# Attention values in blocks of four queries: 512-column products, a dense upper half and a spread lower half

## The chip, the cores and the metric

The kernel runs on one core of one Trainium2 chip. The metric is the device time of one execution in microseconds. A core has five engines that run their own instruction queues: PE (TensorE, matrix products and transposes), DVE (VectorE), ACT (ScalarE), POOL (GpSimd) and SP (SyncE, here only issuing DMAs). PE reads SBUF and writes PSUM, which has eight banks of 128 partitions by 512 fp32 columns.

## The reference

One layer of a hybrid decoder, on 1024 tokens of width 1024: a pre-norm, one wide input product, two groups of heads beside each other (eight heads of differential softmax attention, four heads of gated linear attention), an output product, a post-norm and the residual. The part that matters here is the differential attention:

```python
def diff_attention(q, k, v, lam):          # q,k: (B,S,H,2,64); v: (B,S,H,128)
    q = q * (DA_HEAD_DIM ** -0.5)
    def block(args):                       # one block of 128 queries
        qb, bi = args
        s = jnp.einsum('bqhmd,bkhmd->bhmqk', qb, k)
        mask = key_pos[None, :] <= q_pos[:, None]
        p = jax.nn.softmax(jnp.where(mask, s, -jnp.inf), axis=-1)
        w = p[:, :, 0] - lam * p[:, :, 1]
        return jnp.einsum('bhqk,bkhv->bqhv', w, v)
...
oa = rms_norm(oa, subln_g) * (1.0 - lam_init)
oa = oa.reshape(B, S, DA_WIDTH) * jax.nn.silu(ga)
...
y = jnp.einsum('bse,ed->bsd', jnp.concatenate([oa, ob], axis=-1), w_out)
return x + rms_norm(y, post_g)
```

## The kernel before, in words

Each fp32 product is done as three products of rounded parts (high x high, low x high, high x low). A "split" makes the two parts of a tile: ACT copies the high part, DVE subtracts it from the tile for the low part.

The first two thirds of the kernel make the projections, the gated attention, and the split weights of the output product, and leave them in DRAM. The last third, from about 637 us, is the attention stage. It is written as three streams of PE work, and `merge` interleaves them:

- `all_scores` takes the eight heads in turn and in each the eight query blocks from 7 down to 0. `scores(h, qb)` multiplies queries with keys for both maps (tile `sc`, three PSUM banks), DVE adds the mask and takes the row's extreme (L1167, with the accumulator read beside it), ACT takes the exponential (L1177), DVE the reciprocal of the row sums (L1202), POOL scales the second map (L1203), and DVE forms the weights, first map minus second (L1207). They lie in `p0`, one buffer for each query block, and `w[h, qb]` is set when that is written in the program.
- `all_values` takes the eight heads in turn. `values(h, j)` handles query blocks 2j and 2j+1 for j = 3, 2, 1, 0: `turn(g)` transposes the weights of two key tiles on PE into one of two banks (`wtr`), ACT and DVE split them (`wt_hi` L1244, `wt_lo` L1245), and `times(g)` multiplies them with the values' parts into `po`. A turn is written one turn ahead of its products. ACT copies `po` to `o`. `attn_norm` then squares `o`, splits the square, sums it over partitions by a product with ones (`ms`, in a bank of the transposes), scales by the gate and sends it to DRAM (`mixd`). It is mingled with the turns that follow.
- `out_early` multiplies what is already there with the output weights (`ypart`), as a filler, and later starts the last row tiles (`yps`).

All matmuls and transposes are issued in the order in which they are written (`tc.keep_in_program_order`). The order on the other engines is chosen by the compiler's scheduler. The merge keeps a clock for each stream: a stream has a begin, an end and a total cost, each `yield c` moves its clock by c/cost of its length, and the stream with the lowest clock goes next. A yielded function is a condition: the stream rests until it holds. The values of a pair wait for its lower block in `w`; the scores of block qb of the next head wait until the last turn of the pair that reads the same buffer has been written (`used`). Scores run from 0 to T = 288 units, 36 a head, values from LAG = 21 to T + LAG, the output products from -6 to T + LAG.

Of the kernel before, what the change touches and what calls it, by code (L numbers as in the profile page):

```python
# [14 lines left out]
P = 128  # L15
# [5 lines left out]
DA_HEADS = 8  # L21
# [10 lines left out]
def hymba_kernel(  # L32
# [21 lines left out]
    act, dve, pool, pe, sp = nc.scalar, nc.vector, nc.gpsimd, nc.tensor, nc.sync  # L54

    def fp(t):
        return t.bitcast(F32)

    def cols(half):
        return slice(half * 512, half * 512 + 512)  # L60
# [37 lines left out]
    def bank(i, shape, name):  # L98
        return psum.tile(shape, F32, tag=f"b{i}", name=name)
# [10 lines left out]
    def mm(*a, **k):  # L110
        tc.keep_in_program_order(pe.matmul(*a, **k))  # L111

    def tr(dst, src):
        tc.keep_in_program_order(pe.transpose(dst, src, ident))  # L114
# [867 lines left out]
    def chain(*streams):  # L982
        for st in streams:
            yield from st

    def load_qk(h, n, half):

        if h % 2 and (n == "k" or half):
            t = smps[0].tile([P, 2, 512], F32R, tag=f"{n}{half}", name=f"{n}{half}")
        else:  # L990
            t = kp.tile([P, 2, 512], F32R, tag=f"{n}{half}", name=f"{n}{half}")
        d = qk_d["k" if n == "k" else "q"][h][:, :, :, cols(half)]
        if n != "qs":
            sp.dma_start(fp(t), d.rearrange("m t p s -> (t p) m s"))
        else:
            for i in range(2):
                sp.dma_start(fp(t[64 * i : 64 * i + 64]), d[:, 1 - i].rearrange("m p s -> p m s"))
        qk[h, n, half] = t
# [73 lines left out]
    SC, TR, PO, Y = order_b[:3], order_b[3:5], order_b[5], order_b[6:]  # L1072
# [43 lines left out]
    def load_v(h):  # L1116
        v = [smp.tile([P, NT, P], F32R, tag="v", name=f"v{t}", bufs=4) for t in range(2)]
        for t in range(2):
            ins = sp.dma_start(fp(v[t]), v_d[h // 4][t, h % 4])
            if h == 0:  # L1120
                tc.keep_in_program_order(ins)
        return v
# [9 lines left out]
    def tr_bank(name, shape):  # L1132
        n_tr[0] += 1
        return bank(TR[n_tr[0] % 2], shape, name)


    w, used, scored, opened = {}, set(), [], {}
# [74 lines left out]
    def all_scores():  # L1212
        for h in range(DA_HEADS):
            for qb in range(NT - 1, -1, -1):
                if qb % 2 and h:
                    yield lambda h=h, qb=qb: (h - 1, qb // 2) in used
                yield from scores(h, qb)
                if qb == NT - 1 and h + 1 < DA_HEADS:
                    for n, half in (("q", 1), ("k", 0), ("k", 1), ("qs", 1)):
                        load_qk(h + 1, n, half)  # L1220
            if h + 1 < DA_HEADS:
                for n in ("q", "qs"):
                    load_qk(h + 1, n, 0)
        for _ in range(3):
            scale_scores(None)
        scored.append(True)
        opened.update(dict.fromkeys(SC))

    def values(h, j, v, o):

        yield lambda: (h, 2 * j) in w
        po = bank(PO, [P, 256], "po")

        def turn(g):

            n = 512 if g < j else 384
            pt = tr_bank("wtr", [P, 512])
            for c in range(0, n, P):
                t, i = (c // 256, c % 256 // P) if c < 256 or g < j else (1, 1)
                kt = 2 * g + t  # L1240
                tr(pt[:, c : c + P], w[h, 2 * j + i][:, kt * P : (kt + 1) * P])
            hi = smp.tile([P, 512], F32R, tag="wt_hi", name="wt_hi", bufs=3)
            lo = smp.tile([P, 512], F32R, tag="wt_lo", name="wt_lo", bufs=3)
            act.copy(hi[:, :n], pt[:, :n])  # L1244
            dve.tensor_tensor(lo[:, :n], pt[:, :n], fp(hi[:, :n]), ALU.subtract)  # L1245
            return hi, lo

        def times(g, wt):
            hi, lo = wt
            for i, t in ((0, 0), (1, 0), (0, 1), (1, 1), (2, 0), (2, 1)):  # L1250
                a, b = ((v[0], hi), (v[1], hi), (v[0], lo))[i]
                kt = 2 * g + t
                ns = 256 if kt <= 2 * j else P
                mm(
                    po[:, 256 - ns :], a[:, kt, :], b[:, 256 * t : 256 * t + ns],
                    start=(kt == 0 and i == 0), stop=(kt >= 2 * j and i == 2),
                    skip_group_check=True,
                )

        ready = []  # L1260
        for g in range(j + 1):
            ready.append((g, turn(g)))
            if g == j:
                used.add((h, j))
            yield 0.5
            if len(ready) > 1:
                times(*ready.pop(0))
                yield 0.5
        if j == 0:
            yield 0.5  # L1270
        times(*ready.pop(0))
        act.copy(o[:, j % 2 * 256 : j % 2 * 256 + 256], po)
        yield 0.5

    def attn_norm(h, half, o):
        if h < DA_HEADS - 1:
            gate = smp.tile([P, 512], F32, tag="gate", name="gate", bufs=2)
        else:
            gate = kp.tile([P, 512], F32, tag=("q1", "k1")[half], name="gate")
        sp.dma_start(gate, g_d[h][:, cols(half)])  # L1280
        sq = smp.tile([P, 512], F32, tag="r", name="sq", bufs=1)
        act.activation(sq, o, AF.Square)
        hl = smp.tile([P, 2, 512], F32R, tag="sq_hl", name="sq_hl", bufs=1)
        act.copy(hl[:, 0], sq)
        dve.tensor_tensor(hl[:, 1], sq, fp(hl[:, 0]), ALU.subtract)
        yield 0.0
        yield 0.0
        n_tr[0] += 1
        ms = bank(TR[n_tr[0] % 2], [P, 512], "ms")
        for i in range(2):  # L1290
            mm(ms, ones, hl[:, i], start=(i == 0), stop=(i == 1))
        if h == DA_HEADS - 1 and not half:
            opened[TR[n_tr[0] % 2]] = None
        r = smp.tile([P, 512], F32, tag="r", name="r", bufs=1)
        act.activation(r, ms, AF.Ln, bias=eps_t, scale=1.0 / P)
        act.activation(r, r, AF.Exp, scale=-0.5)
        dve.scalar_tensor_tensor(r, o, sub_g, r, ALU.mult, ALU.mult)
        dst = o if h < DA_HEADS - 1 else gate
        pool.tensor_tensor(dst, r, gate, ALU.mult)
        if h < DA_HEADS - 1:  # L1300
            sp.dma_start(mixd[h * P : (h + 1) * P, cols(half)], o)
            stored.append(h)
        else:
            last_mix[half] = gate
        yield 0.0

    def mingle(a, b):

        a, b = iter(a), iter(b)
        for c in a:  # L1310
            yield c
            if callable(c):
                continue
            c = next(b, None)
            if c is not None:
                yield c
        yield from b

    def all_values():
        carry = iter(())  # L1320
        nxt = v_first
        for h in range(DA_HEADS):
            v = nxt
            o = [smp.tile([P, 512], F32, tag="o", name="o", bufs=3) for _ in range(2)]
            yield from mingle(values(h, 3, v, o[1]), carry)
            if h + 1 < DA_HEADS:
                nxt = load_v(h + 1)
            yield from values(h, 2, v, o[1])
            yield from mingle(
                chain(values(h, 1, v, o[0]), values(h, 0, v, o[0])), attn_norm(h, 1, o[1])  # L1330
            )
            carry = attn_norm(h, 0, o[0])
        last_part(ENDS[0], parts_d[ENDS[0]])
        yield next(carry)
        yield lambda: (ENDS[2], 0) in ps_d
        early_ends()
        yield from carry
# [32 lines left out]
    def times(ps, part, e0, dh, e, last):  # L1370
        mh, ml = part
        hi, lo = wo[e]
        for i, (a, b) in enumerate(((mh, hi), (ml, hi), (mh, lo))):
            mm(
                ps, a[:, e - e0, :], b[:, cols(dh)],
                start=(e == e0 and i == 0), stop=(e == last and i == 2),
            )
# [123 lines left out]
    def last_times(st, dh, part, e):  # L1501
# [6 lines left out]
            )  # L1508

    T = 8 * 36.0  # L1510
    LAG = 21.0
    s_cost = sum(
        2 * sum(0.08 + (min(b, n) - a) / 512 * 0.56 for a, b in parts_of(n)) + 0.25 + n / 1024 * 1.4
        for n in range(P, S + 1, P)
    )
    merge(
        [0.0, T, DA_HEADS * s_cost, all_scores()],
        [LAG, T + LAG, DA_HEADS * 10.5, all_values()],
        [-6.0, T + LAG, 11.0 + 14 * 5.52 + 16 * 2.76 + 11.8, out_early()],
    )  # L1520

# [125 lines left out]
```

## Time and profile before

| | us |
|---|---|
| median of 3 runs | 977.59 |
| lowest, highest run | 977.15, 982.69 |
| profiled execution, its own time | 977.73 |
| its span in the trace | 976.0 |
| PE busy in the span | 956.0 (98%) |
| DVE, ACT, POOL busy | 738.7, 590.9, 211.5 |
| mean granted TensorE clock | 0.998 |

In the rows that follow, a line of a timeline is start, duration, engine, source line, operation, output tile <- input tiles, shape and count, with idle time before it and its releaser in brackets. A line of a group has the count, the busy time in us, the mean duration of one in ns, and the idle time before. `PEld` is the weight load of PE. All matmuls are written in the helper at L111 and all transposes in the one at L114, so they are told apart by tile names.

### The profile page before, as it was taken

What the parts mean: (1) busy time and instruction counts of PE and PEld (TensorE: products, weight loads), DVE (VectorE), ACT (ScalarE), POOL (GpSimd) and SP (SyncE); (2) the same over time, 40 slices, a digit from 0 to 9 for tenths busy, and PEclk for the clock granted to TensorE, in tenths of its full rate; (3) what the DMA queues carried; (4) which work ended last, traced back from release to release, by engine and by line L of the source; (5) the groups of instructions that cost most, each with busy time, mean ns of one, the idle gap of its engine ahead of it and who ended that gap; (6) DMA issues with size and microseconds to landing.
All of it is one profiled execution on the core that took longest, in us unless ns stands there. A gap on an engine that the chain in (4) does not pass through costs nothing.

```text
span 976.0 us, 14803 instructions
## 1 busy us (share of the span) xinstructions
PE 956.0 (98%) x4866; PEld 806.1 (83%) x4866; DVE 738.7 (76%) x1450; ACT 590.9 (61%) x1152; POOL 211.5 (22%) x289
## 2 busy tenths in 40 slices
PE   6999999999999999999999999999999999999997
PEld 4888888878888888888888888788888888888875
DVE  6996476889889776778787766577787778887655
ACT  8641232347467467766677774357667667787764
POOL 5420100011211221112110000023232233443232
PEclk9999999999999999999999999999999999999999
DMA  8354643768865875899986569997575678995657
GB/s 306 99 152 153 212 134 98 217 174 270 265 240 194 268 250 192 265 280 304 315 278 183 180 204 346 376 337 233 164 252 185 189 267 246 331 262 104 194 157 156
DMA packets 144556, 220.37 MB, mean 226 GB/s; under 512 B 14704, under 2 KB 78704, under 8 KB 144384
## 3 DMA queue, kind: packets, MB, share of 16 engines
q1 hardware_dynamic: 130144, 175.38, 56.6%
q0 software_dynamic: 14336, 44.05, 15.1%
q8 instruction: 38, 0.62, 0.3%
q14 instruction: 38, 0.31, 0.1%
HBM read 133.93 MB, written 88.60 MB: 228 GB/s over the span
## 4 chain that ended last, share of the span: by engine, by line
PE 86%; DMA 6%; DVE 3%; ACT 3%; issue 1%; SPq 1%; DVEq 0%; POOL 0%; ACTq 0%
PE v L111 15%; PE x L111 15%; PE ypart L111 11%; PE y L111 10%; PE z L111 10%; PE sc L111 6%; PE po L111 5%; PE yps L111 4%; PE wtr L114 3%; PE gpo L111 2%; PE kv L111 1%; DMA m_raw<-mixd 1%; DMA m_lo<-mixe 1%; DMA mixd<-o 1%; DMA k_d<-qk_st 1%
## 5 line engine op out<-in xcount | busy, mean ns | idle before, releaser
L1177 ACT ACTIVATE p<-p,stt 128x896 f32<-128x896 f32 (+7 forms) x128 | 99.3, 777 | 46.7 <-DVE stt L1167 43.5
L335 DVE TENSOR_TENSOR w<-w_raw,w 128x512 fp32r<-128x512 f32 x134 | 91.9, 690 | 32.5 <-ACT w L333 32.1
L333 ACT CAST w<-w_raw 128x512 fp32r<-128x512 f32 x134 | 82.5, 620 | 42.9 <-PE y L111 19.9
L1203 POOL TENSOR_SCALAR p<-p,stt,lam 128x1024 f32<-128x1024 f32 (+3 forms) x64 | 55.7, 871 | 209.6 <-DVE stt L1202 203.9
L1167 DVE CUSTOM_DVE_ANT_0 p<-sc,maskt 128x512 f32<-128x512 f32 (+3 forms) x128 | 74.4, 585 | 33.2 <-PE sc L111 32.5
L111 PE MATMUL y<-h_hi,w 128*128 128x512 f32 x320 | 80.6, 394 | 0.0
L111 PE MATMUL x<-s_hi,w 128*128 128x512 f32 x320 | 80.5, 394 | 0.0
L111 PE MATMUL z<-s_hi,w 128*128 128x512 f32 x320 | 80.4, 393 | 0.0
L111 PE MATMUL ypart<-wo_hi,m_hi 128*128 128x512 f32 x192 | 79.5, 414 | 0.6 <-ACT yst L1384 0.5
L111 PE MATMUL v<-w,s_hi 128*128 128x512 f32 x256 | 79.0, 389 | 0.1
L111 PE MATMUL ypart<-wo_hi,m_lo 128*128 128x512 f32 x192 | 75.6, 394 | 0.7 <-DMA m_lo<-mixe 0.7
L111 PE MATMUL ypart<-wo_lo,m_hi 128*128 128x512 f32 x192 | 75.6, 394 | 0.5 <-DMA wo_lo<-wo_d 0.5
L488 ACT COPY s<-x 128x512 f32<-128x512 f32 x60 | 35.0, 584 | 65.2 <-PE x L111 65.0
L111 PE MATMUL sc<-k,q 128*128 128x512 f32 (+1 forms) x192 | 70.9, 372 | 0.4 <-DVE stt L1167 0.4
L111 PEld LDWEIGHTS z<-s_hi,w 128*128 128x128 f32 x320 | 59.1, 188 | 11.6
L111 PEld LDWEIGHTS x<-s_hi,w 128*128 128x128 f32 x320 | 59.1, 188 | 11.7
L111 PEld LDWEIGHTS y<-h_hi,w 128*128 128x128 f32 x320 | 59.0, 188 | 11.6
L111 PE MATMUL sc<-k,qs 128*128 128x512 f32 (+1 forms) x192 | 66.6, 349 | 0.0
L285 ACT CAST w<-w_block 128x1024 fp32r<-128x1024 f32 x24 | 25.0, 1051 | 65.3 <-PE v L111 42.3
L257 DVE TENSOR_TENSOR w_raw<-w_raw 128x512 f32<-128x512 f32 x80 | 55.3, 691 | 9.6 <-DMA w_raw<-in_w_in_dram 8.6
L111 PE MATMUL v<-w,h_hi 128*128 128x512 f32 x192 | 60.0, 400 | 0.4 <-ACT h_hi L582 0.4
L1207 DVE SCALAR_TENSOR_TENSOR p<-p,stt,p 128x1024 f32<-128x1024 f32 (+3 forms) x64 | 52.3, 819 | 6.7 <-POOL p L1203 6.5
(233 smaller groups left out, 2379.8 us busy)
## 6 DMA issues: line engine op xcount, KB each, us to landing
w_raw<-in_w_in_dram SPq DMA_DIRECT2D x40, 512.0 KB, 4.9
w_block<-in_w_in_dram SPq DMA_DIRECT2D x16, 512.0 KB, 4.4
wo_raw<-in_w_out_dram POOLq DMA_DIRECT2D x32, 256.0 KB, 4.2
wo_d<-wo_hi POOLq DMA_DIRECT2D x32, 256.0 KB, 4.5
wo_d<-wo_raw POOLq DMA_DIRECT2D x32, 256.0 KB, 5.0
qs<-q_d SPq DMA_DIRECT2D x32, 256.0 KB, 8.6
k<-k_d SPq DMA_DIRECT2D x16, 512.0 KB, 9.2
q<-q_d SPq DMA_DIRECT2D x16, 512.0 KB, 7.1
```

The source lines that it names most:

```text
L111: tc.keep_in_program_order(pe.matmul(*a, **k))
L114: tc.keep_in_program_order(pe.transpose(dst, src, ident))
L257: dve.tensor_tensor(dst, a, b, ALU.subtract)
L285: act.copy(w[0], src)
L333: act.copy(w[0], src)
L335: split_last[:] = [dve.tensor_tensor(w[1], src, fp(w[0]), ALU.subtract)]
L488: act.copy(b[k], ps)
L1167: ins = dve.tensor_tensor_reduce(p[:, a:e], sc[:, : e - a], maskt[:, NZ + P - (e - a) :] if last else maskt[:, : e - a], 1.0, 3e38 if i == ...
L1177: act.activation(p[:, :n], p[:, :n], AF.Exp, bias=st[:, m : m + 1], scale=-1.0, accum_out=st[:, 2 + m : 3 + m],)
L1203: pool.tensor_scalar(p1[:, :n], p1[:, :n], st[:, 5:6], lam, ALU.mult, ALU.mult)
L1207: dve.scalar_tensor_tensor(p0[:, :n], p0[:, :n], st[:, 4:5], p1[:, :n], ALU.mult, ALU.subtract)
```

## The change

The values now take four query blocks at a time. `values(h, half)` handles blocks 4·half to 4·half+3, upper half first. A turn transposes one key tile of up to four query blocks, 512 columns, and its products are three matmuls of up to 512 columns into a `po` of 512 columns. Towards the end of a half, where keys lie behind the first query blocks, they shrink to 384, 256 and 128 columns. The conditions follow: values wait for block 4·half, scores of blocks 7 and 3 wait for the upper and lower half of the head before.

The costs of the streams are rewritten: the values' total cost is T, so that a yield's cost is in the merge's own units. The upper half's 16 steps take DENSE = 11 units together, the lower half's 8 steps the other 25 of a head's 36. In the last head every step takes 1.2. LAG goes from 21 to 27. The normalization of the upper half is mingled with the lower half, that of the lower half with the next head's upper half; the next head's values are loaded behind the upper half.

```diff
-                if qb % 2 and h:
-                    yield lambda h=h, qb=qb: (h - 1, qb // 2) in used
+                if qb % 4 == 3 and h:
+                    yield lambda h=h, qb=qb: (h - 1, qb // 4) in used
...
-    def values(h, j, v, o):
-        yield lambda: (h, 2 * j) in w
-        po = bank(PO, [P, 256], "po")
+    def values(h, half, v, o, cost):
+        yield lambda: (h, 4 * half) in w
+        po = bank(PO, [P, 512], "po")
+        last = 4 * half + 3
-        def turn(g):
-            n = 512 if g < j else 384
+        def turn(kt):
+            first = max(kt - 4 * half, 0)
+            n = 512 - first * P
             pt = tr_bank("wtr", [P, 512])
-            for c in range(0, n, P):
-                t, i = (c // 256, c % 256 // P) if c < 256 or g < j else (1, 1)
-                kt = 2 * g + t
-                tr(pt[:, c : c + P], w[h, 2 * j + i][:, kt * P : (kt + 1) * P])
+            for i in range(first, 4):
+                c = (i - first) * P
+                tr(pt[:, c : c + P], w[h, 4 * half + i][:, kt * P : (kt + 1) * P])
...
-        def times(g, wt):
-            hi, lo = wt
-            for i, t in ((0, 0), (1, 0), (0, 1), (1, 1), (2, 0), (2, 1)):
-                a, b = ((v[0], hi), (v[1], hi), (v[0], lo))[i]
-                kt = 2 * g + t
-                ns = 256 if kt <= 2 * j else P
+        def times(kt, wt):
+            hi, lo, n = wt
+            for i, (a, b) in enumerate(((v[0], hi), (v[1], hi), (v[0], lo))):
                 mm(
-                    po[:, 256 - ns :], a[:, kt, :], b[:, 256 * t : 256 * t + ns],
-                    start=(kt == 0 and i == 0), stop=(kt >= 2 * j and i == 2),
+                    po[:, 512 - n :], a[:, kt, :], b[:, :n],
+                    start=(kt == 0 and i == 0), stop=(kt == last and i == 2),
                     skip_group_check=True,
                 )
         ready = []
-        for g in range(j + 1):
-            ready.append((g, turn(g)))
-            if g == j:
-                used.add((h, j))
-            yield 0.5
+        for kt in range(last + 1):
+            ready.append((kt, turn(kt)))
+            if kt == last:
+                used.add((h, half))
+            yield cost
             if len(ready) > 1:
                 times(*ready.pop(0))
-                yield 0.5
-        if j == 0:
-            yield 0.5
+                yield cost
         times(*ready.pop(0))
-        act.copy(o[:, j % 2 * 256 : j % 2 * 256 + 256], po)
-        yield 0.5
+        act.copy(o, po)
+        yield cost
...
-            yield from mingle(values(h, 3, v, o[1]), carry)
+            yield from mingle(values(h, 1, v, o[1], DENSE / 16 if h + 1 < DA_HEADS else 1.2), carry)
             if h + 1 < DA_HEADS:
                 nxt = load_v(h + 1)
-            yield from values(h, 2, v, o[1])
             yield from mingle(
-                chain(values(h, 1, v, o[0]), values(h, 0, v, o[0])), attn_norm(h, 1, o[1])
+                values(h, 0, v, o[0], (36.0 - DENSE) / 8 if h + 1 < DA_HEADS else 1.2),
+                attn_norm(h, 1, o[1]),
             )
...
-    LAG = 21.0
+    LAG, DENSE = 27.0, 11.0
...
-        [LAG, T + LAG, DA_HEADS * 10.5, all_values()],
+        [LAG, T + LAG, T, all_values()],
```

More of the change, by code (lines that the diff above doesn't have):

```diff
@@ L1245, in turn @@
             dve.tensor_tensor(lo[:, :n], pt[:, :n], fp(hi[:, :n]), ALU.subtract)
-            return hi, lo
-        def times(g, wt):
-            hi, lo = wt
-            for i, t in ((0, 0), (1, 0), (0, 1), (1, 1), (2, 0), (2, 1)):
-                a, b = ((v[0], hi), (v[1], hi), (v[0], lo))[i]
-                kt = 2 * g + t
-                ns = 256 if kt <= 2 * j else P
-                mm(
-                    po[:, 256 - ns :], a[:, kt, :], b[:, 256 * t : 256 * t + ns],
-                    start=(kt == 0 and i == 0), stop=(kt >= 2 * j and i == 2),
+            return hi, lo, n
+        def times(kt, wt):
+            hi, lo, n = wt
+            for i, (a, b) in enumerate(((v[0], hi), (v[1], hi), (v[0], lo))):
+                mm(
+                    po[:, 512 - n :], a[:, kt, :], b[:, :n],
+                    start=(kt == 0 and i == 0), stop=(kt == last and i == 2),
                     skip_group_check=True,
```

## The prediction

> **What bounds the kernel now.** I read the page's head first, then the chain that ended last, then the stretches of one attention head each, then PE's own waits.
>
> ```profile
> span 976.0 us, 14803 instructions
> PE 956.0 (98%) x4866; PEld 806.1 (83%) x4866; DVE 738.7 (76%) x1450; ACT 590.9 (61%) x1152; POOL 211.5 (22%) x289
> ...
> PE 86%; DMA 6%; DVE 3%; ACT 3%; issue 1%; SPq 1%; DVEq 0%; POOL 0%; ACTq 0%
> ```
>
> PE is busy from end to end and carries 86% of the chain. The stage that changes is the attention:
>
> ```profile
> 674.90:712.70 37.80, 37.69 (x223) 32.76 (x222) 28.32 (x79) 25.84 (x58) 11.84 (x14) 1.00 0.66 199
> 712.70:750.20 37.50, 37.50 (x222) 32.72 (x221) 28.64 (x80) 25.90 (x58) 10.88 (x13) 1.00 0.63 207
> 826.40:864.00 37.60, 37.60 (x222) 32.70 (x221) 31.16 (x85) 28.66 (x63) 19.42 (x25) 1.00 0.98 288
> ```
>
> The columns are the stretch, its length, then busy time of PE, weight loads, DVE, ACT and POOL, the granted clock and DMA. A head takes 37.6 us; PE is busy in all of it, DVE for 28.3 to 31.2, ACT for 25.8 to 28.7. PE's waits in the stage are single events:
>
> ```profile
> PE po L111 <- ACT wt_hi L1244: 0.6, 1, 0.6
> PE ypart L111 <- ACT yst L1384: 0.5, 1, 0.5
> PE wtr L114 <- ACT r L1295: 0.4, 1, 0.4
> PE sc L111 <- DVE stt L1167: 0.4, 1, 0.4
> ```
>
> So time falls only if PE's own work falls, and rises by whatever PE is made to wait: its instructions keep their written order, so one late operand holds scores, values and output products alike.
>
> **PE's work.** A matmul's row gives its latency; what it costs is the distance to the next start.
>
> ```profile
> 714.43 0.60 PE L114 MATMUL wtr<-ident,p 128*128 128x128 f32 x4
> 714.78 0.48 PE L111 MATMUL ypart<-wo_hi,m_hi 128*128 128x512 f32 x1
> 715.10 0.39 PE L111 MATMUL ypart<-wo_hi,m_lo 128*128 128x512 f32 x1
> 715.33 0.40 PE L111 MATMUL ypart<-wo_lo,m_hi 128*128 128x512 f32 x1
> 715.56 0.64 PE L111 MATMUL po<-wt_hi,v 128*128 128x256 f32 x4
> 716.04 0.40 PE L111 MATMUL po<-wt_lo,v 128*128 128x256 f32 x2
> 716.28 0.39 PE L111 MATMUL ypart<-wo_hi,m_hi 128*128 128x512 f32 x1
> ...
> 720.88 0.34 PE L111 MATMUL sc<-k,q 128*128 128x384 f32 x1
> 721.06 0.34 PE L111 MATMUL sc<-k,qs 128*128 128x384 f32 x1
> ...
> 773.27 0.58 PE L111 MATMUL po<-wt_hi,v 128*128 128x256 f32 x4
> 773.68 0.39 PE L111 MATMUL po<-wt_lo,v 128*128 128x256 f32 x2
> 773.92 0.45 PE L111 MATMUL sc<-k,q 128*128 128x512 f32 x1
> ```
>
> A 512-column matmul costs 0.23 us (715.10 to 715.33). A 384-column one costs 0.18 (720.88 to 721.06). A full group of six 256-column products takes 0.72 (715.56 to 716.28), 0.12 each: exactly half. The last group of a pair, three of 256 and three of 128 columns alternating (773.27 to 773.92), takes 0.65: 0.108 each, so a 128-column product costs nearly what a 256-column one does. Four transposes and the lengthened step behind them (714.43 to 715.10, less 0.23) take 0.44, 0.11 each.
>
> Before, a head has 6 full groups and 4 last ones: 6 x 0.72 + 4 x 0.65 = 6.9 us, 60 products. After, 18 products of 512 columns, and 6 each of 384, 256 and 128: 18 x 0.23 + 6 x (0.18 + 0.12 + 0.108) = 6.6 us. That is 24 products fewer, on the same 13,824 columns; the gain is only where 128-column products stood between wider ones, 0.3 us a head, **2.4 us in all**. If the narrow ones in a row cost half of 0.12, it is 4.7; I take 2.4. The 36 transposes a head stay, at the same 0.11.
>
> **ACT, DVE and queues.** The splits go from 10 to 12 a head over the same 4,608 columns; two more ACT casts and DVE subtractions cost only their fixed part. The copies out of the sum's bank go from four of 256 to two of 512 columns. All lie under PE, at nothing, as ACT has 12 us free a head and DVE 6 to 9. No DMA is added; loading the next head's values moves behind the upper half, 25 merge units (the merge's own time, 36 a head) before it is needed, so SP's queue gives it cover. If these covers fail, the price is in the waits below.
>
> **Waits that go.** PE's four waits above come to 1.9 us, and around 910 us it loses some more behind these steps:
>
> ```profile
> 909.26 0.52 ACT m_hi L1469
> 909.80 1.03 DVE m_lo L1470 x2
> 910.83 0.60 DVE p L1167
> 911.44 0.80 DVE p L1207
> 912.24 0.60 DVE wt_lo L1245
> ```
>
> There the chain runs on DVE behind a tile that arrived late from head 6's upper half. Its normalization now comes about 6 us of PE's work earlier, as it stands in the first turns of the lower half. I take 2.5 off, between 0 and 4.
>
> **The wait that comes.** Before, the first transposes of a head read blocks 6 and 7, scored long before; block 4 is first read by the second pair, about 12 us of PE's work after its scores. After, the first transpose of a head reads block 4, the last one the scores delivered. By the merge's costs blocks 7 to 4 take 14.1 of a head's 20.3, so their scores end at 25.0 of 36 units. The values begin at 27.0. A larger LAG would not open this: scores of the next head are let in only after the eighth turn, 13/16 x 11 = 8.9 units later, so both shift together and 36 - 25.0 - 8.9 = 2.1 units remain, plus the 2.4 of the last score step itself. Walking that order, PE has between block 4's last scores and the first transpose three output triples (3 x 0.69), two score pairs of block 3 (2 x 0.46) and the last narrow products (0.32), with its own step 3.4 us (2.7 for head 1).
>
> What must happen in that time is one chain. Here it is for block 4 of head 1 before:
>
> ```profile
> 676.48 0.28 PE L111 MATMUL sc<-k,qs 128*128 128x256 f32 x1
> ...
> 679.21 0.34 DVE L1167 CUSTOM_DVE_ANT_0 p<-sc,maskt,stt 128x128 f32<-128x128 f32 x1
> ...
> 679.59 0.83 ACT L1177 ACTIVATE p<-p,stt 128x640 f32<-128x640 f32 x1 [1.77 <-DVE stt L1167]
> ...
> 680.55 0.17 DVE L1202 RECIPROCAL stt<-stt 128x2 f32<-128x2 f32 x1
> ...
> 680.89 0.88 POOL L1203 TENSOR_SCALAR p<-p,stt,lam 128x640 f32<-128x640 f32 x1 [5.08 <-DVE stt L1202]
> ...
> 682.50 0.88 DVE L1207 SCALAR_TENSOR_TENSOR p<-p,stt,p 128x640 f32<-128x640 f32 x1
> ```
>
> From the score matmul (676.48) to the finished weights (683.38) it took 6.9 us, with 2.5 of it before DVE came round. The durations alone are 0.28 + 0.34 + 0.83 + 0.17 + 0.88 + 0.88 = 3.4; half a microsecond comes on top, as DVE must first reduce the 512 columns of the same map, and some 0.3 between engines: 4.2. So PE waits at each head's first transpose for at least 4.2 - 3.4 = 0.8 us and, with the queue of before, 3.5. In the spread stretch DVE has fewer value splits in the way, so I take **1.5**, nearer the bare end. Behind the waiting transpose stand the output products, which need nothing and now wait too.
>
> **The dense turns.** Before, a turn and its products lie 3 to 5.7 us apart in PE's work. Now the first lies 1.5, the later ones 2.1 to 3.7; in the last head 1.4 to 4.3. A split took, before:
>
> ```profile
> 680.78 0.60 PE L114 MATMUL wtr<-ident,p 128*128 128x128 f32 x4
> ...
> 681.85 0.57 ACT L1244 CAST wt_hi<-wtr 128x512 fp32r<-128x512 f32 x1
> ...
> 683.30 0.68 DVE L1245 TENSOR_TENSOR wt_lo<-wtr,wt_hi 128x512 fp32r<-128x512 f32 x1
> ```
>
> 3.2 us from the transposes' start to the low part; bare it is 0.60 + 0.57 + 0.68 = 1.85. The third product of the first group needs the low part 2.0 after the start: a wait of 0 to 1.2, I take **0.6** a head for it. The normalization of the head before also stands there, its sum 2.2 us after its three operations on ACT and DVE; its wait lies mostly inside the first one. Later turns I cost at nothing, up to 0.3 each.
>
> **Sum.** 8 heads x (1.5 + 0.6) = 16.8, less 2.4 and 2.5: +11.9. The profiled execution took 977.73 (span 976.0), the median of the runs shown is 977.59, so the same: 977.7 + 11.9 = **989.6, say 989**. Ends: 8 x 0.8 - 4.7 - 4 = -2 (975); 8 x (3.5 + 1.2) - 2.4 = +35 (1013).
>
> **The rivals.**
> *The chain fits, no change* (0.41). DVE and ACT come round to the urgent operands in time; PE waits under 0.8 us a head, 6 us in all or nothing. For it: DVE idles 6 to 9 us a head, and bare chain and distance differ by under 1 us. Against: in none of the rows was the chain bare. It gives 977.7 - 4.9 + 0 to 14, that is 973 to 987. If the narrow products and all old waits are saved and nothing comes, 969.
>
> *The wait dominates* (in the forecast's chance, its far end, 0.08 of it). The chain stays at 6.9 and the dense turns crowd DVE: 1004 to 1013. It decides as soon as the chain exceeds 3.4 by more than 3 us.
>
> *Wide products are cheaper than their columns* (0.04), the other side.
>
> ```profile
> L111 PE MATMUL po<-wt_hi,v 128*128 128x256 f32 x256 | 43.3, 281 | 0.6 <-ACT wt_hi L1244 0.6
> L111 PE MATMUL po<-wt_lo,v 128*128 128x256 f32 x128 | 30.7, 301 | 0.3
> ...
> L111 PE MATMUL po<-wt_hi,v 128*128 128x128 f32 x64 | 10.7, 249 | 0.0
> ...
> L111 PE MATMUL po<-wt_lo,v 128*128 128x128 f32 x32 | 7.1, 223 | 0.0
> ```
>
> If the durations (281, 301, 249, 223 ns, against 390 to 400 for 512 columns in the rows above) were the costs, a head's products would fall from 16.7 to about 12.4 us: 35 us less, 943. Against it stand the starts: 0.23 for 512 columns, 0.12 for 256. [...] The rival keeps a small chance.
>
> **How the numbers follow.** A measurement of this kernel tells about 1% from no change. Slower by more than that (above 987.4) has 0.55: it needs added waits over 1.8 us a head, and my two terms give 2.1. Within 1% has 0.41, faster (under 967.9) 0.04. The range 974 to 1004 leaves out some 0.12 below and 0.08 above.
>
> **What would show it.** Right: PE rows with idle time at the first transpose of each head, released by DVE at L1207's operation (the line numbers move), 1 to 3 us each, eight times, and shorter ones at the values' products; products of 512 columns 0.23 apart, and their sum with the narrow ones about 6.6 us a head; heads 39 to 40 us long. Wrong: the first transposes follow without a gap, heads of 37.3 us, and the end near 973; or the waits stand elsewhere, at the normalization's sum or the bank of the sums, which I cost at nothing.

## The result and the profile after

The changed kernel takes 1005.14 us in the median (1002.0 to 1011.77) against 979.54 for the kernel before beside it: 1.0264 times as long, with an interval of 1.0223 to 1.0304. The profiled execution took 1002.0, its span is 24.3 us longer than before. The forecast had the sign and the mechanism, and less than half of the size; the median lies 1 us past the end of its range.

The page's head and the chain that ended last, of the changed kernel:

```profile
span 1000.3 us, 14452 instructions
...
PE 957.9 (96%) x4674; PEld 797.8 (80%) x4674; DVE 749.2 (75%) x1466; ACT 589.1 (59%) x1152; POOL 209.1 (21%) x289
...
PE 83%; DVE 5%; ACT 3%; issue 3%; DMA 3%; POOL 2%; SPq 0%; DVEq 0%; POOLq 0%; ACTq 0%
```

PE has 192 matmuls fewer and is busy for as long as before, 957.9 against 956.0, because some of them now run slowly (below). What is new is 22 us in which it is not busy. The chain shows whose they are: DVE, ACT and POOL rise from 6% to 10% of it.

PE's waits in the attention stage (engine, tile, line, releaser, then sum, count and longest):

```profile
PE wtr L114 <- DVE p L1207: 23.5, 11, 5.7
PE po L111 <- ACT wt_hi L1245: 1.1, 3, 0.6
PE po L111 <- DVE wt_lo L1246: 0.2, 1, 0.2
```

One line carries it: transposes that wait for DVE's combined weights, the row that the prediction named. In the order of time the eleven waits are 1.46, 1.11, 2.73, 0.18, 0.54, 2.36, 2.52, 3.10, 0.93, 2.89 and 5.66. Eight stand at the first transpose of an upper half, 21.3 us together, 2.7 a head; three, 2.2 us together, at the first transpose of a lower half (1.11, 0.18 and 0.93). Two heads by windows, in the columns of the prediction:

```profile
683.10:722.00 38.90, 38.00 (x196) 31.25 (x196) 29.14 (x79) 24.31 (x54) 10.74 (x13) 1.00 0.58 184
842.70:885.30 42.60, 38.80 (x196) 32.64 (x196) 30.76 (x84) 28.31 (x63) 17.79 (x22) 0.96 0.93 254
```

Heads of 37.4 to 38.5 us became 38.9 to 42.6. Block 4's chain of head 1, the one that the prediction priced, in the timeline of the changed kernel (start, duration, engine, line):

```profile
677.50 0.28 PE L111 MATMUL sc<-k,qs 128*128 128x256 f32 x1
...
678.29 1.02 DVE L1207 SCALAR_TENSOR_TENSOR p<-p,stt,p 128x768 f32<-128x768 f32 x1 [0.20 <-POOL p L1203]
...
679.22 0.35 DVE L1167 CUSTOM_DVE_ANT_0 p<-sc,maskt,stt 128x128 f32<-128x128 f32 x1
...
679.61 0.83 ACT L1177 ACTIVATE p<-p,stt 128x640 f32<-128x640 f32 x1
...
680.90 0.87 POOL L1203 TENSOR_SCALAR p<-p,stt,lam 128x640 f32<-128x640 f32 x1 [2.65 <-DVE stt L1202]
681.24 1.07 DVE L1281 TENSOR_TENSOR sq_hl<-sq,sq_hl 128x512 fp32r<-128x512 f32 x1
682.24 0.87 DVE L1207 SCALAR_TENSOR_TENSOR p<-p,stt,p 128x640 f32<-128x640 f32 x1
...
683.16 0.66 PE L114 MATMUL wtr<-ident,p 128*128 128x128 f32 x4 [2.73 <-DVE p L1207]
```

From the score matmul to the finished weights 5.6 us pass (677.50 to 683.11). Two pieces of DVE's queue lie in it: block 5's combination, 1.02 long, in front of the reduction, and the subtraction of the normalization (L1281), which holds DVE until 682.3 when POOL has been done since 681.77. PE ran out of work at 680.4 (683.16 less 2.73). In the last head the chain is longer still, 9.3 us from the score matmul (918.59) to the first transpose. Two operations for the output product, waiting for a tile from DMA, stand ahead of it on ACT and DVE:

```profile
922.82 0.93 ACT L1465 CAST m_hi<-m_raw 128x384 fp32r<-128x384 f32 x2 [1.90 <-DMA m_raw<-mixd]
...
923.36 1.03 DVE L1466 TENSOR_TENSOR m_lo<-m_raw,m_hi 128x384 fp32r<-128x384 f32 x2 [1.57 <-ACT m_hi L1465]
...
927.87 1.11 PE L114 MATMUL wtr<-ident,p 128*128 128x128 f32 x4 [5.66 <-DVE p L1207]
```

And a wait can cost more than its length. Behind head 5's, 512-column matmuls start 0.42 apart (844.09 to 844.51), not 0.23:

```profile
842.74 1.12 PE L114 MATMUL wtr<-ident,p 128*128 128x128 f32 x4 [3.10 <-DVE p L1207]
843.51 0.78 PE L111 MATMUL ypart<-wo_hi,m_hi 128*128 128x512 f32 x1
844.09 0.63 PE L111 MATMUL ypart<-wo_hi,m_lo 128*128 128x512 f32 x1
844.51 0.63 PE L111 MATMUL ypart<-wo_lo,m_hi 128*128 128x512 f32 x1
```

The distances in the stage beyond those of full speed add up to about 4.3 us, against 0.5 before. The stage took 302.0 us before (637 to 939) and 326.0 after (637 to 963). Of these 24.0 us, PE was idle in 22.9 (25.0 against 2.1) and busy in 1.1, where 3.8 of slow matmuls and -2.5 of products make 1.3.

### The profile page after: what moved, and what is told of

It reads as the page before. It is cut to its first block, busy times and chain, and to the rows that moved or that the text cites. A ratio compares the mean times of both kernels' runs of the same rounds, so it can differ in the third digit from the quotient of the medians.

```text
span 1000.3 us, 14452 instructions
## 1 busy us (share of the span) xinstructions
PE 957.9 (96%) x4674; PEld 797.8 (80%) x4674; DVE 749.2 (75%) x1466; ACT 589.1 (59%) x1152; POOL 209.1 (21%) x289
## 4 chain that ended last, share of the span: by engine, by line
PE 83%; DVE 5%; ACT 3%; issue 3%; DMA 3%; POOL 2%; SPq 0%; DVEq 0%; POOLq 0%; ACTq 0%
PE x L111 16%; PE v L111 15%; PE y L111 11%; PE z L111 10%; PE ypart L111 8%; PE sc L111 5%; PE yps L111 4%; PE po L111 4%; PE wtr L114 3%; PE gpo L111 2%; DVE p L1167 1%; PE kv L111 1%; DVE p L1207 1%; ACT p L1177 1%; POOL p L1203 1%
## 5 line engine op out<-in xcount | busy, mean ns | idle before, releaser
L1203 POOL TENSOR_SCALAR p<-p,stt,lam 128x1024 f32<-128x1024 f32 (+3 forms) x64 | 53.2, 832 | 207.6 <-DVE stt L1202 127.5
L1246 DVE TENSOR_TENSOR wt_lo<-wtr,wt_hi 128x512 fp32r<-128x512 f32 (+1 forms) x96 | 52.8, 555 | 28.0 <-ACT wt_hi L1245 27.6
L114 PE MATMUL wtr<-ident,p 128*128 128x128 f32 x288 | 49.5, 286 | 23.5 <-DVE p L1207 23.5
L111 PE MATMUL sc<-k,q 128*128 128x512 f32 (+1 forms) x192 | 68.7, 360 | 0.1
L111 PEld LDWEIGHTS y<-h_hi,w 128*128 128x128 f32 x320 | 59.0, 188 | 11.6
L114 PEld LDWEIGHTS wtr<-ident,p 128*128 128x128 f32 x288 | 37.1, 147 | 34.4 <-DVE p L1207 26.1
```

The lines of the kernel that those rows point to most:

```text
L1203: pool.tensor_scalar(p1[:, :n], p1[:, :n], st[:, 5:6], lam, ALU.mult, ALU.mult)
```

## The experiments

The theory after the result, called A in the expectations: block 4's weights are late at the first transposes. The rival, B: the packing of an upper half's steps into 11 units itself crowds ACT and DVE, wherever block 4 stands. A third, C: 512-column products are dearer than they look.

**More distance, and less.** `LAG, DENSE = 33.0, 11.0` gives the merge six units more between the scores and the first transpose, `25.0, 11.0` two units less.

> The changed kernel with LAG at 33 in place of 27; nothing else. In PE's own work the first transpose of a head then stands 7.1 us behind the last scores of block 4, not 3.4. Theory A (the weights of block 4 come late, PE waits for them): the 22.6 us of waits at the first transposes fall under 4, and with them the slow clock behind them; 977 to 984 us. Theory B (eight turns packed into 11 units crowd ACT and DVE): the packing is the same, so 1000 to 1006. Theory C (512-column products are dearer than they look): the same, 1000 to 1006.

> The changed kernel with LAG at 25. The first transpose of a head then stands 1.2 us behind the last scores of block 4 (1.5 or 0.8, by head), 2.2 less than with 27. A: each of eight heads waits 2.2 us longer, less 0.7 for head 0 whose values cannot open earlier: 15 to 18 us more, 1018 to 1024. B and C: no change, 1000 to 1008.

At 25, 1030.83 us against 978.21 for the kernel before: 1.0542 [1.0527, 1.0558], longer than A's figure; the mean granted clock of the profiled execution is 0.98 there, against 0.991 at 27, so not all of it is waits. At 33, 989.28: 1.0125 [1.0095, 1.0155], above A's. PE's waits of the two, LAG 25 first:

```profile
PE wtr L114 <- DVE p L1207: 39.1, 14, 5.8
```

```profile
PE po L111 <- ACT wt_hi L1245: 8.9, 6, 2.6
PE po L111 <- DVE wt_lo L1246: 1.2, 5, 0.4
...
PE wtr L114 <- DVE p L1207: 0.2, 1, 0.2
```

The same wait grows to 39.1 and shrinks to 0.2 with the distance alone: A's cause is shown. But 10 us of waits came up one step later, at the first products, where PE waits for ACT's split of the transposed weights. Taking A's waits away brings back half of the loss. Head 4's, in the timeline with LAG 33:

```profile
799.29 0.60 PE L114 MATMUL wtr<-ident,p 128*128 128x128 f32 x4
...
800.30 0.62 ACT L1356 CAST m_hi<-m_raw 128x512 fp32r<-128x512 f32 x1 [1.54 <-issue]
800.82 0.61 ACT L1280 CAST sq_hl<-sq 128x512 fp32r<-128x512 f32 x1
...
801.85 0.56 ACT L1245 CAST wt_hi<-wtr 128x512 fp32r<-128x512 f32 x1
...
802.46 0.73 PE L111 MATMUL po<-wt_hi,v 128*128 128x512 f32 x2 [2.58 <-ACT wt_hi L1245]
```

The transposes end at 799.9; ACT then does a cast for the output product, which it begins at 800.30 (the profile names no releaser for the 1.54 us of idle time before it), the normalization's split of the head before and an exponential, and reaches `wt_hi` 2 us late.

**Another way to the same end.** Key tiles are taken last to first, so the first transpose of an upper half reads block 7, and block 4 stands in the later ones:

```
for kt in range(last, -1, -1):   # and start at kt == last, stop at kt == 0
```

> The changed kernel with the key tiles of each half taken from the last to the first: the first turn of the upper half reads block 7 alone, the second 6 and 7, the fourth is the first that reads block 4, five steps or some 4 us of PE's work later. Same products, same packing, same LAG. A: the waits at the first transposes go, 975 to 983, since the narrow products and the wide ones are all still there and save 2.5. B: the same packing, 1000 or over. C: 1000 or over.

990.64: 1.0130 [1.0100, 1.0159], above A's 975 to 983. No transposes wait here, and again the first products do (1.0 us of waits at the normalization's sum come on top):

```profile
PE po L111 <- ACT wt_hi L1245: 5.1, 4, 2.6
PE po L111 <- DVE wt_lo L1246: 4.2, 7, 1.0
```

Two different edits that both let block 4 be read later bring the ratio from 1.0264 to 1.0125 and 1.0130, the same within their intervals, and leave the same second half.

**Pairs under the new timing.** The products of before, two blocks at a time, with the new clock (upper half dense, lower half spread, LAG 27):

```
up, low = (DENSE / 14, (36.0 - DENSE) / 7) if h + 1 < DA_HEADS else (1.2, 1.2)
```

> The kernel before with the new timing alone: pairs of query blocks and 256-column products as before, but the two upper pairs' 14 steps in 11 units, the two lower ones' 7 steps in 25, LAG 27, 1.2 a step in the last head. Block 4 is first read by the second pair, eight steps or 6.3 units later. A: no wait at first transposes, 978 to 986. B: dense turns cost by themselves, 990 to 1003. C: like A, 978 to 986; against keys_down it then shows what the shape is worth.

983.19: 1.0058 [1.0041, 1.0076], as A said. The dense timing costs some 5 us with the blocks in pairs too, and at the same place:

```profile
PE po L111 <- DVE wt_lo L1245: 5.0, 7, 1.4
PE po L111 <- ACT wt_hi L1244: 2.6, 3, 1.3
```

So the waits at the products don't need halves of four blocks: they come with the dense turns, and to that extent B holds. Halves of four under this timing cost the rest (1.0058 to 1.0264, some 20 us), and there the wait is block 4's.

**One link less.** POOL's scaling of block 4 is left out (`if qb != 4:` before it).

> The changed kernel without POOL's scaling of the second map for query block 4 (it leaves lambda and the second normalization out of that block); all else as it is, with the same matmuls, packing and LAG. It takes 0.88 us of POOL and two hand-overs out of the chain from block 4's scores to its weights. A (late weights): each of eight waits is 1.0 to 1.4 us shorter, 8 to 11 us off the changed kernel, 991 to 997 us. B (packing) and C (shape): POOL is not their engine, so 1000 to 1006.

994.77: 1.0175 [1.0136, 1.0214], inside A's range. The waits at the transposes halve:

```profile
PE wtr L114 <- DVE p L1208: 11.9, 9, 3.5
```

Nothing of PE's was touched; a link of 0.87 us taken from the chain took 11.6 us of waits away there, more than its 8 x 0.87, and brought the ratio from 1.0264 to 1.0175, some 9 us. The waits at products rose from 1.3 to 3.0 us. The trace is of the fastest of its four executions (987.94 to 999.19), in which the granted clock was 0.998, not 0.991; so its span is shorter by more, 14.1 us.

**The second half.** Three tries with LAG 33. The first delays the normalization of the head before by four steps of the merge; the second orders its operations behind the first split on ACT and DVE; the third takes away what holds the casts for the output product (it loads them from an input, not from the attention's stored output), with a control that does the same to the kernel before.

```
carry = chain(iter([0.0] * (4 if h + 1 < DA_HEADS else 0)), attn_norm(h, 0, o[0]))   # late_norm
with tc.issue_after(splits[0].ins): act.activation(sq, o, AF.Square)                 # pin_norm, and L1281
md = w_out[0, :D, :].rearrange("(e p) s -> p e s", p=P)                              # no_store
```

> The changed kernel with LAG 33, and the lower half's normalization of the head before begun four steps later, so that its square, split and subtraction no longer stand on ACT and DVE beside the first turn's split. Theory D (what is left with LAG 33 is the first split, queued on ACT and DVE behind the normalization and behind the loads of the output products): in heads 1 to 3, where the normalization alone is in the way, the waits at the first products (1.4, 0.35, 0.35 us) go; in heads 4 to 6, where ACT's cast of a tile from DRAM is ahead, most of 7 us stay. 2 to 5 us less than with LAG 33, 984 to 988. If the packing of DVE as a whole holds PE, no change, 988 to 991.

> LAG 33 again, now with the lower half's normalization truly moved: its square is ordered on ACT, and its subtraction on DVE, behind the split of the next head's first turn. (Written later in the program alone, as in the run before, it was moved forward again on those engines.) D: the first products of heads 1 to 3 wait 1.4, 0.35 and 0.35 us less, and those of heads 4 to 6 lose the 0.6 to 1.2 us of square and split; 3 to 5 us less than with LAG 33, 985 to 988, unless the sum over the squares, which PE needs four steps later, now comes late itself. If DVE's load as a whole holds PE, 988 to 992.

> LAG 33, but the tiles of stored attention outputs that the output products load are read from an input of the same shape in place of the store, so that no load waits for a store (the output leaves the attention out of these products). D: in heads 4 to 6 ACT's cast and DVE's subtraction of these tiles no longer stand waiting ahead of the first split, and some 5 of 7 us of waits at the first products go, in the last head 1 to 2 more: 982 to 986. If the packing itself is what holds PE there, no change, 988 to 992.

> The control: the kernel before with the same substitution. Its only longer waits behind such a load are those around 910 us and two short ones, 2 us: 975 to 977. So what the substitution saves beyond 2 us with LAG 33 belongs to the changed timing.

*late_norm*: 991.64, 1.0122 [1.0089, 1.0156], no change, where 984 to 988 were expected. It tested nothing: the square still comes 2.6 us ahead of the first split on ACT (679.68 against 682.28), as with LAG 33 alone (685.47 against 688.08). The compiler's scheduler orders ACT's work, and writing the operation later in the program did not move it.

*pin_norm*: 991.46, 1.0118 [1.0085, 1.0152], no change either, where 985 to 988 were expected, but its waits did move:

```profile
PE po L111 <- ACT wt_hi L1246: 5.8, 4, 2.2
PE ms L111 <- DVE sq_hl L1287: 2.6, 5, 0.7
```

In head 1 the 0.89 us in front of the first products become 0.20, but PE now waits 0.59 at `ms`, the normalization's sum, and 0.65 and 0.61 in the next two heads: its split comes later, and the sum still stands two steps behind it in PE's order. The long waits of heads 4 and 5 stay (2.06 and 2.22, where LAG 33 alone has 2.58 twice).

*no_store*: 986.01, 1.0079 [1.0054, 1.0104], but the control lost as much the other way: 985.13, 1.0069 [1.0044, 1.0093], where 975 to 977 were expected, with a 3.0 us wait at one product and 1.8 for values from DMA. So the substitution is not neutral, and the pair doesn't decide. Head 4's wait falls from 2.58 to 0.41 with it, those of heads 5 and 6 stay at 2.59 and 1.56. With LAG 33 alone, what stands ahead of the split in head 5 is not such a load: ACT copies a finished piece of the output product (`yst`) at 841.89, after 0.74 us of waiting for an earlier store of that buffer to land, then does the square and an exponential, and reaches `wt_hi` at 843.40, 2 us behind the transposes. In head 6 the same operations stand there without a wait for DMA.

**Both causes together.** Keys last to first, each turn waiting for its own block alone (`yield lambda kt=kt: (h, max(kt, 4 * half)) in w`), with the start of the values and the length of the dense part shifted: LAG 24 with DENSE 16, LAG 22 with DENSE 20, and LAG 24.5 with DENSE 14 and the pin above.

> Key tiles from the last to the first, each turn waiting only for the blocks that it reads, LAG 24 and the upper half's 16 steps in 16 units in place of 11 (1.0 a step). Block 4 is then read some 5.9 us of PE's work behind its scores and the turns stand 3.1 to 3.9 us ahead of their products, not 2.1 to 2.9. A with D: both kinds of wait are mostly gone, and 2.5 us are saved by the products: 974 to 980, at or under the kernel before. B as a cost of four-block halves in themselves: still 985 or more.

> The same with LAG 22 and 20 units for the upper half (1.25 a step). Block 4 is read 4.8 to 5.4 us behind its scores, a little more than the chain takes when nothing is queued (4.2) and less than it took at most (7.2), the products stand 3.4 to 5.4 us behind their turns. A with D: waits at first products go, some at block 4 come back, up to 1 us a head: 973 to 983. B: 985 or more.

> The version that the runs point to: key tiles from the last to the first, each turn waiting only for the blocks that it reads, LAG 24.5 and 14 units for the upper half, so that the next head's scores are not held back (24.5 + 13/16 x 14 = 35.9 of 36), and the normalization ordered behind the first split. A with D: no wait at transposes, the first split early; what is left are loads from the store in heads 4 to 7, some 6 us: 978 to 983. To beat the kernel before it would have to lose those too.

LAG 24: 985.36, 1.0063 [1.0040, 1.0086], above the 974 to 980 expected and at B's figure; its waits stand at products and scores, none at the normalization's sum. LAG 22: 995.33, 1.0146 [1.0116, 1.0177], far above the 973 to 983 expected. By the merge's units its DENSE of 20 holds the next head's scores back (22 + 13/16 x 20 = 38.3 of 36); no run shows that this is the cause. LAG 24.5 with the pin: 983.54, 1.0050 [1.0033, 1.0067], just past the 978 to 983 expected, and its waits stand at the normalization's sum:

```profile
PE ms L111 <- DVE sq_hl L1287: 3.4, 6, 1.2
PE ms L111 <- ACT sq_hl L1285: 1.7, 2, 1.0
```

Head 1 of it in the timeline, where the sum's second matmul follows the subtraction at once:

```profile
678.78 0.85 DVE L1287 TENSOR_TENSOR sq_hl<-sq,sq_hl 128x512 fp32r<-128x512 f32 x1
...
679.68 0.50 PE L111 MATMUL ms<-sq_hl,ones 128*128 128x512 f32 x1 [0.30 <-DVE sq_hl L1287]
```

That named the last edit: five steps of the merge, not two, between the normalization's split and its sum, in all lower halves but the last; once with the pin and once without.

```
for _ in range(2 if half or h == DA_HEADS - 1 else 5):
    yield 0.0
```

> Key tiles from the last to the first, LAG 24.5, 14 units for the upper half, the normalization ordered behind the first split, and its sum over the squares three steps (some 3 us of PE's work) later. If only its place was in the way: the 5.1 us of waits at that sum go and 2 us of transposes behind it, 976 to 979, level with the kernel before or a little under it. If the packing as such holds PE, the waits move on to splits and scores: 981 to 985.

> The same without the order behind the first split: the normalization runs as early as it can on ACT and DVE, its sum three steps later. Place alone: first splits wait some 0.5 us a head behind square and subtraction, no wait at the sum, 979 to 983. Packing: 982 to 986.

With the pin 976.79 against 978.36: 0.9992 [0.9974, 1.0009], inside the 976 to 979 expected. Without it 977.05: 0.9979 [0.9962, 0.9996], better than the 979 to 983 expected. One edit, 6.7 us (983.54 to 976.79), and the loss is gone; with the sum later, the pin is worth nothing. The pin itself may have brought some of the waits that this edit took away: with LAG 33 it raised those at the sum from 0 to 2.6 us. The version with neither pin nor later sum was not run, so how the 8 us between 985.36 and 977.05 divide between the sum's place and the shift of LAG and DENSE stays open. The timeline and PE's waits of the version without the pin:

```profile
679.01 1.18 DVE L1281 TENSOR_TENSOR sq_hl<-sq,sq_hl 128x512 fp32r<-128x512 f32 x1 [0.34 <-ACT sq_hl L1280]
...
683.59 0.62 PE L111 MATMUL ms<-sq_hl,ones 128*128 128x512 f32 x2
```

```profile
PE sc L111 <- DVE stt L1167: 1.2, 1, 1.2
PE po L111 <- DVE wt_lo L1245: 1.1, 2, 0.7
PE po L111 <- ACT wt_hi L1244: 0.8, 2, 0.5
```

The subtraction is done at 680.19, and the sum starts at 683.59. What is left is single waits, some 4 us in the stage against 2 before, which take most of the 2.5 us that the products save: the version is level with the kernel before, or 0.2% under it. It has four blocks at a time, the same splits and a head like this:

```profile
678.00:716.00 38.00, 37.61 (x201) 31.61 (x200) 29.46 (x80) 26.11 (x60) 10.80 (x13) 1.00 0.67 215
```

DVE is busy for 29.5 of 38 us, and PE is idle for 0.4. So halves of four blocks cost nothing in themselves. Whether the density matters is not settled: this version spreads the upper half over 14 units, and none with 11 was run with the later sum.

## Why the prediction was right or wrong

**PE's work: right.** Products of 512, 384, 256 and 128 columns start as priced. Two rows of the changed kernel's timeline and what follows them:

```profile
693.98 0.62 PE L111 MATMUL po<-wt_hi,v 128*128 128x512 f32 x2
694.44 0.40 PE L111 MATMUL po<-wt_lo,v 128*128 128x512 f32 x1
694.67 0.28 PE L111 MATMUL sc<-k,q 128*128 128x256 f32 x1
```

Three take 0.69, 0.23 each. By medians of each group's length, a head's products cost 6.84 before and 6.53 after: 2.5 in eight heads, where 2.4 were taken. Wide products are not cheaper than their columns, nor dearer; that rival is out, and C with it.

**The wait that comes: right place, wrong size.** This is the step that failed: "I take 1.5, nearer the bare end". The distance was right: PE had its own work for 2.9 us in head 1, where 2.7 were walked, and for 3.6 in the heads behind it, where 3.4 were. But the chain from the score matmul to the first transpose took 5.7, 5.7, 4.1, 6.0, 6.2, 6.7, 6.5 and 9.3 us in the eight heads. Only head 2 was near the bare 4.2, and 21.3 us stood where 8 x 1.5 = 12 were put. The reason given held as far as it went: the value splits that stood in DVE's way before (676.80 and 678.61) are gone from head 1's chain. But the previous block's combination and the normalization's subtraction stand in it, and in the last head a subtraction that waits for a DMA came in. The normalization's was there before too, between the two splits and ahead of the reduction:

```profile
678.00 0.69 DVE L1285 TENSOR_TENSOR sq_hl<-sq,sq_hl 128x512 fp32r<-128x512 f32 x1
```

So most heads lay between the bare sum and the 6.9 of before, nearer to the 6.9.

**Costed at nothing, and not nothing.** The lower halves' first transposes wait 2.2, by the same mechanism (their block 0 is the last one scored). The slow matmuls behind the long waits cost 3.8. The prediction priced a wait by its length only. Its "fixed part" of a split can be read from the changed kernel's rows: `wt_hi` took 0.58, 0.48, 0.37 and 0.26 us on average at 512, 384, 256 and 128 columns, `wt_lo` 0.69, 0.55, 0.42 and 0.29, so some 0.15 us of each does not go with its columns.

**The dense turns: hidden, then found.** The products' waits were to be 0.6 a head, 4.8; after, they are 1.3 in all; DVE and ACT can catch up while PE waits for block 4. With that wait gone, they are 10.1 (LAG 33): twice the term. The two terms don't add; the second stands behind the first, which is why A's figures for LAG 33 and for the keys last to first were missed. "Its wait lies mostly inside the first one", said of the normalization's sum, held too: there is no wait at the sum in the changed kernel, nor with LAG 33, but 1.0 us with the keys last to first and more in three of the later versions (2.6, 5.1 and 5.4).

**A larger LAG: wrong.** "A larger LAG would not open this: both shift together" overlooked that a stream held by a condition keeps its own due time. LAG sets the distance: 7.1 us of PE's work at LAG 33 in head 1, and the waits go.

**The waits that go: right in the main.** Those near 910 us are gone; the term was 2.5, and the four rows of before come to 1.9.

Put with the measured sizes, the sum is 21.3 + 2.2 + 1.3 + 3.8 - 2.5 - 1.9 = 24.2, against the 11.9 forecast; the stage grew by 24.0. Open: what the later sum would do without the keys' order, and which part of the last versions' gain is the looser timing's.

## What to carry to other kernels

When a change moves a consumer next to its producer's last result, price the chain with the queue that stands on each engine at that moment, taken from the rows of before, and look at which of those operations stay in it. Waits in series hide one another: name what is late next before counting a removed wait as gained. If a wider shape costs time, look for the one dependency that it brought forward; here the keys' order, the timing and the later sum together gave all of it back, while the shape itself was worth only what PE's starts said, 2.5 us.

## What the runs showed of the hardware

**Behind three of the eleven waits PE's granted clock was halved, behind the other eight it was not.** Rows of the changed kernel, eight transposes each behind a wait of about the same length:

```profile
801.65 1.97 PE L114 MATMUL wtr<-ident,p 128*128 128x128 f32 x8 [2.52 <-DVE p L1207]
```

```profile
885.36 1.09 PE L114 MATMUL wtr<-ident,p 128*128 128x128 f32 x8 [2.89 <-DVE p L1207]
```

The shorter wait was followed by transposes at half speed (1.62 us from the first of them to the matmul behind them, against 0.84, and 512-column matmuls 0.42 apart until 804.7), the longer one was not; waits of 3.10 and 5.66 were, waits of 2.73 and 2.36 were not. The granted clock was 0.50 from 801.5 to 804.9, from 842.5 to 845.9 and from 924.4 to 931.2, and 1.00 in the rest of the stage: slow stretches of 3.41, 3.41 and 6.83 us. Their starts are 41.0 and then 81.9 us apart, 12 and 24 times 3.41. In the 3.41 us just before each of them PE was busy for only 1.0, 0.6 and 1.2 us. With steps of 3.41 counted on from the first start (an estimate from these three), the wait of 2.89 fell across two of them, with PE busy for 2.5 and 1.5 us, and the clock stayed. So the length of a wait alone did not decide; what does, three stretches are too few to show.

**DVE's subtraction of two tiles in SBUF took longer beside POOL's arithmetic.** At 512 columns, alone with LAG 33 (first fence) and beside two operations of POOL in its variant with the loads from an input:

```profile
800.95 0.69 DVE L1357 TENSOR_TENSOR m_lo<-m_raw,m_hi 128x512 fp32r<-128x512 f32 x1 [1.98 <-ACT m_hi L1356]
```

```profile
827.80 1.66 POOL L1295 TENSOR_TENSOR o<-r,gate 128x512 f32<-128x512 f32 x1
829.09 1.22 POOL L1203 TENSOR_SCALAR p<-p,stt,lam 128x640 f32<-128x640 f32 x1
829.10 1.75 DVE L1357 TENSOR_TENSOR m_lo<-m_raw,m_hi 128x512 fp32r<-128x512 f32 x1 [0.23 <-ACT m_hi L1356]
```

0.69 became 1.75: the subtraction ends at 830.85, 0.54 behind POOL's scaling (830.31). In the chain of head 1 above, the normalization's subtraction took 1.07 and ended 0.54 behind the scaling too (682.31 against 681.77), while the scaling kept its 0.87. The changed kernel's attention stage has 24 such subtractions: three overlap a scaling of POOL and took 0.85, 1.07 and 1.49, the other 21 took 0.68 to 0.69. The longest in the kernel before took 1.91, beside POOL's product with the gate (824.56 to 826.23); one of 384 columns there kept its 0.55 beside a scaling (914.90). The subtractions for `wt_lo`, which read a PSUM tile, did not lengthen: of the changed kernel's 48 at 512 columns, 18 overlap a scaling or a gate product of POOL and took 0.68 to 0.69. What in the engines makes the difference is not shown. The chain that set the loss has both kinds of operation in it.
